# Four more FFN units by half-size products, token sums beside the first half, and low weight parts by adding transfers

## The chip, the cores and the metric

One core of one Trainium2 chip runs the whole model in one launch. The metric is the device time of that launch in microseconds (us). The kernel before takes 1629.13 us, the median of 3 runs (1628.31 to 1630.39). Every time in this document that is read from a profile comes from one profiled execution.

## The reference, cut to what matters

Two layers act on 256 latent tokens (LAT) and 256 context tokens (CTX) of width 1024. Layer 0 is a half FFN, an attention and a half FFN; layer 1 a half FFN, an mLSTM and a half FFN. Each part is followed by a layer norm, and each is modulated by vectors that come from products with `ada_w`.

```python
def half_ffn(h, shift, scale, gate, w_in, w_out, g, b):
    xm = modulate(h, shift, scale)
    a, u = jnp.split(xm @ w_in, 2, axis=-1)
    y = (jax.nn.silu(a) * u) @ w_out
    return post_norm(h, 0.5 * gate * y, g, b)
...
    for i in range(DEPTH):
        mod_lat = jnp.split((jax.nn.silu(c) @ ada_w[i] + ada_b[i])[:, None, :], N_MOD, axis=-1)
```

`w_in` is 1024 x 5632 and `w_out` 2816 x 1024, all float32. The output is the latent part of the last norm.

## The kernel before

The stages run one after the other: FFN 0, attention, FFN 1 (the second), FFN 2 (the third), mLSTM, last FFN. The change touches the second and the third, both `ffn` with `li` 1 and 2.

**Products.** A float32 product is made of three matmuls of a faster type: each operand is split into a high and a low part, and `mm3` (L241) issues high x high, high x low and low x high. `split` makes the parts of a tile: the high one by a cast on ScalarE (ACT, L225), the low one by a subtraction on VectorE (DVE, L230). `raw` (L210) loads a 512 KB chunk of weights by SP's queue into one of 3 slots, `pair` takes one of 7 tiles for both parts, and `chunk` does all three.

**An FFN.** The 2816 hidden columns are 22 units of 128, in two halves of 11; a unit has a silu side and a plain side, two chunks of `w_in`. Units 0 to 3 (the lead) run first for LAT and then for CTX, beside the end of the norm before. Units 4 to 10 are plain: 48 matmuls of 512 columns each. Then the out half 0 adds the eleven units' share to all 8 output blocks d (`unit_out`, 33 matmuls each). The second half, units 11 to 21, is fast: `fast_in` computes each unit by seven half-size products in place of eight (12 matmuls of 256 columns each, 84 in all), with `a11`, `a12`, `a21`, `a22` the quarters of the unit's weights. It needs four sums of quarters (`s1`, `s2`, `s4`, `s3`, L641, in one tile `sums`) and their splits, and three sums of halves of the tokens, which `fast_sums` (L611 to L623) makes for all fast units at once, beside d = 4 and 5 of the out half 0 (`SUMSAT`). One of these sums overwrites the CTX part of the lower half of `xh` and `xl`, which no plain unit reads any more by then. The out half 1 follows, its last four blocks (the tail) first for LAT and then for CTX, so that the next norm can begin.

**Dots.** The modulation vectors are dots on VectorE (`ada_dot`, L350): a 512 KB piece of `ada_w`, in one of 4 buffers, against two vectors (layer 1's last pieces against one). `DOTS` says how many pieces are loaded after each unit and each block; the dots of the pieces loaded at one such place are issued at the next (`flush`). `residual` (L563, L564) rescales the stream's blocks, two per unit.

**Order.** The Tile scheduler fixes one order for each engine and places the waits. An engine takes its instructions strictly in that order. So what stands ahead of an instruction on its own engine delays it even where the two have nothing to do with each other.

Of the kernel before, what the change touches and what calls it, by code (L numbers as in the profile page):

```python
# [18 lines left out]
P = 128  # L19
# [42 lines left out]
S1B = 5  # L62
# [26 lines left out]
SUMSAT = 4  # L89
# [53 lines left out]
class Stream:  # L143


    def __init__(self, b, chunks, sh=0):
        self.b, self.chunks, self.kept = b, chunks, (None, None)
        self.sh = sh if callable(sh) else lambda c: sh

    def __call__(self, i, w=P):  # L150
        c, o = divmod(i * P, 1024)
        if self.kept[0] != c:
            self.kept = (c, self.b.chunk(self.chunks[c], self.sh(c)))
        h, l = self.kept[1]
        return h[:, o : o + w], l[:, o : o + w]


class Keep(Stream):


    def __init__(self, b, chunks, sh=0, seen=None):
        super().__init__(b, chunks, sh)
        self.all = dict([seen.kept]) if seen else {}

    def __call__(self, i, w=P):
        c, o = divmod(i * P, 1024)
        if c not in self.all:
            self.all[c] = self.b.chunk(self.chunks[c], self.sh(c))
# [4 lines left out]
class Body:  # L173
    def __init__(self, ctx, tc, a, out):
# [8 lines left out]
        self.nraw, self.spare = 0, None  # L183

# [33 lines left out]
    def chunk(self, src, sh=0):  # L218
        r = self.raw(src)
        h, l = self.pair(sh=sh)  # L220
        self.split(r, h, l)
        return h, l

# [65 lines left out]
    def silu_c(self):  # L289

        pool = ExitStack()
        self.n += 1
        p = pool.enter_context(self.tc.tile_pool(name=f"cp{self.n}", bufs=1, side="right"))
        self.cp = p
        self.cb = self.t([P, 2, D], pool=p)
        return pool
# [5 lines left out]
    def silu_all(self):  # L302
        pool = self.silu_c()
        self.silu_load()
        self.silu()
        return pool
# [33 lines left out]
    def ada_load(self, layer, dt):  # L340
        if (layer, dt // ND) not in self.mod:
            self.mod[layer, dt // ND] = self.t([P, 2, ND])
        r = self.t([P, 1024], tag="ada", bufs=PIECES, pool=self.cp)
# [248 lines left out]
    def fast_operands(self, st):  # L592

        n = ND // 2 * TL
        x = self.t([P, 6 * n], F32R, pool=st)
        self.t([P, FLIP], pool=st)
        self.made = [[x[:, (2 * i + p) * n : (2 * i + p + 1) * n].rearrange("p (k f) -> p k f", f=TL) for p in range(2)] for i in range(3)]

    def fast_sums(self, i):
# [5 lines left out]
        def at(ks, g):  # L605
            return self.xh[:, ks, g[0] : g[1]], self.xl[:, ks, g[0] : g[1]]

        def whole(ks, g):
            o = self.tmp().rearrange("p (k f) -> p k f", k=2)
            h, l = at(ks, g)  # L610
            V.tensor_tensor(out=o, in0=h.bitcast(F32), in1=l.bitcast(F32), op=ALU.add)  # L611
# [3 lines left out]
        V.tensor_tensor(out=a, in0=a, in1=b, op=ALU.subtract)  # L615
        self.split(a, *at(lo, CTX))
# [3 lines left out]
        V.scalar_tensor_tensor(a, a, -1.0, c, ALU.mult, ALU.subtract)  # L620
        self.split(a, *made(0))
        d = whole(up, LAT)
        V.scalar_tensor_tensor(d, a, -1.0, d, ALU.mult, ALU.subtract)  # L623
        self.split(d, *made(2))

    def fast_in(self, j, w_in, st):
# [14 lines left out]
        add = lambda o, x, y: V.tensor_tensor(out=o, in0=x, in1=y, op=ALU.add)  # L641
# [7 lines left out]
        self.split(sums[:, : 2 * half], *ws[2])  # L649
        self.split(sums[:, 2 * half :], *ws[3])  # L650
# [33 lines left out]
    def ffn(self, layer, s, gate, groups, side, start=None, cpool=None):  # L684
# [4 lines left out]
        with self.tc.tile_pool(name=f"ffn{li}", bufs=1) as gp:  # L689
# [33 lines left out]
            stream = lambda j: Stream(self, [w_in[2 * j + i] for i in range(2)])  # L723
            for hf in range(2):
                js = list(range(hf * NFH, (hf + 1) * NFH))[0 if hf else done :]
                if hf == 0 and not start:
                    first = js[:LEAD]
                    ws = {j: Keep(self, [w_in[2 * j + i] for i in range(2)], SH) for j in first}
# [1040 lines left out]
```

## Time and profile before

| | |
|---|---|
| median of 3 runs | 1629.13 us (1628.31 to 1630.39) |
| span of the profiled execution | 1625.5 us |
| time around that span, against the median | 3.6 us |
| TensorE (PE) busy | 1606.9 us, 99% |
| VectorE (DVE) busy | 1355.7 us, 83% |
| ScalarE (ACT) busy | 749.2 us, 46% |
| GpSimd (POOL) busy | 63.0 us, 4% |
| moved by DMA | 251.56 MB |

The span runs from the first to the last recorded instruction. In a row of a timeline stand the start, the duration, the engine, the line of the program, the operation, output and inputs with their sizes, how many such instructions follow each other, and in brackets the idle time before and what ended it. A duration on VectorE or ScalarE overlaps the next instruction a little: the distance between two starts is what an instruction costs.

### The profile page before, as it was taken

What the parts mean: (1) busy time and instruction counts of PE and PEld (TensorE: products, weight loads), DVE (VectorE), ACT (ScalarE), POOL (GpSimd) and SP (SyncE); (2) the same over time, 40 slices, a digit from 0 to 9 for tenths busy, and PEclk for the clock granted to TensorE, in tenths of its full rate; (3) what the DMA queues carried; (4) which work ended last, traced back from release to release, by engine and by line L of the source; (5) the groups of instructions that cost most, each with busy time, mean ns of one, the idle gap of its engine ahead of it and who ended that gap; (6) DMA issues with size and microseconds to landing.
All of it is one profiled execution on the core that took longest, in us unless ns stands there. A gap on an engine that the chain in (4) does not pass through costs nothing. (4 is left out here: it accounts for less than half of the span.)

```text
span 1625.5 us, 26587 instructions
## 1 busy us (share of the span) xinstructions
PE 1606.9 (99%) x10304; PEld 1451.7 (89%) x10304; DVE 1355.7 (83%) x2699; ACT 749.2 (46%) x1272; POOL 63.0 (4%) x77
## 2 busy tenths in 40 slices
PE   9999999999999999999999999999999999999998
PEld 7888888889988998889998998889999989999987
DVE  7899977649889879899986879699966968897687
ACT  6522132314676443316652444336652657566542
POOL 0000000001011100000000100000001000030000
PEclk9999999999999999999999999999999999999999
DMA  9687766422202447633445258713363343437552
GB/s 358 221 252 237 235 205 187 137 66 85 66 1 80 151 134 221 219 117 105 129 146 180 79 165 289 253 58 118 104 225 100 98 130 87 142 110 253 181 176 91
DMA packets 72222, 251.56 MB, mean 155 GB/s; under 512 B 7960, under 2 KB 10776, under 8 KB 72096
## 3 DMA queue, kind: packets, MB, share of 16 engines
q1 hardware_dynamic: 71520, 249.09, 47.7%
q8 instruction: 80, 1.31, 0.3%
q10 hardware_dynamic: 576, 0.79, 0.1%
q14 instruction: 46, 0.38, 0.1%
HBM read 248.79 MB, written 1.05 MB: 154 GB/s over the span
## 5 line engine op out<-in xcount | busy, mean ns | idle before, releaser
L241 PE MATMUL t<-t,t 128*128 128x256 f32 (+2 forms) x8412 | 1317.0, 318 | 6.4 <-ACT t L225 3.3
L241 PEld LDWEIGHTS t<-t,t 128*128 128x128 f32 x8412 | 1185.7, 188 | 125.4 <-ACT t L225 4.7
L225 ACT CAST t<-t 128x1024 fp32r<-128x1024 f32 (+3 forms) x521 | 428.5, 844 | 485.8 <-PE t L241 214.5
L230 DVE TENSOR_TENSOR t<-t,t 128x256 fp32r<-128x256 f32 (+2 forms) x740 | 513.8, 729 | 111.9 <-ACT t L225 107.7
L350 DVE SCALAR_TENSOR_TENSOR t<-t,t 128x1024 bf16<-128x1024 f32 x224 | 260.7, 1220 | 0.0
L588 ACT ACTIVATE t<-t 128x512 f32<-128x512 f32 (+1 forms) x71 | 34.5, 490 | 103.5 <-PE t L241 102.4
L941 PE MATMUL t<-t,t 128*128 128x256 f32 (+1 forms) x256 | 79.3, 310 | 0.0
L718 DVE SCALAR_TENSOR_TENSOR t<-t,t,t 128x256 f32<-128x256 f32 x96 | 42.7, 478 | 43.9 <-PE t L241 43.7
L943 PE MATMUL t<-t,t 128*128 128x256 f32 (+1 forms) x256 | 78.4, 306 | 0.0
L942 PE MATMUL t<-t,t 128*128 128x256 f32 (+1 forms) x256 | 78.4, 306 | 0.0
L589 DVE TENSOR_TENSOR t<-t,t 128x512 f32<-128x512 f32 (+1 forms) x71 | 39.0, 553 | 40.6 <-PE t L241 28.1
L484 POOL TENSOR_TENSOR t<-t,t 128x256 f32<-128x256 f32 x30 | 23.4, 781 | 1104.9 <-ACT t L474 1103.5
L869 PE MATMUL t<-t,t 128*128 128x512 f32 (+1 forms) x300 | 60.5, 364 | 0.0
L869 PEld LDWEIGHTS t<-t,t 128*128 128x128 f32 x300 | 51.5, 189 | 8.9
L474 ACT ACTIVATE t<-t 128x256 f32<-128x256 f32 x72 | 26.1, 412 | 65.5 <-DVE t L467 65.5
L1456 PE MATMUL t<-t,t 128*128 128x512 f32 (+2 forms) x276 | 55.6, 356 | 0.0
L1456 PEld LDWEIGHTS t<-t,t 128*128 128x128 f32 (+1 forms) x276 | 44.9, 183 | 10.9 <-issue 0.9
L942 PEld LDWEIGHTS t<-t,t 128*128 128x128 f32 x256 | 48.1, 188 | 3.0 <-DVE t L230 0.5
L941 PEld LDWEIGHTS t<-t,t 128*128 128x128 f32 x256 | 48.3, 189 | 2.7
L943 PEld LDWEIGHTS t<-t,t 128*128 128x128 f32 x256 | 48.1, 188 | 2.5
L541 ACT ACTIVATE t<-t,t 128x256 fp32r<-128x256 f32 x72 | 32.8, 503 | 30.1 <-DVE t L540 30.1
L641 DVE TENSOR_TENSOR t<-t,t 128x512 f32<-128x512 f32 x66 | 45.2, 685 | 0.4
(206 smaller groups left out, 1078.6 us busy)
## 6 DMA issues: line engine op xcount, KB each, us to landing
t<-in_ffn_in SPq DMA_DIRECT2D x168, 512.0 KB, 4.1
t<-in_ada_w SPq DMA_DIRECT2D x138, 512.0 KB, 4.4
t<-in_ffn_out SPq DMA_DIRECT2D x66, 512.0 KB, 4.5
t<-in_ffn_last SPq DMA_DIRECT2D x22, 512.0 KB, 3.5
t<-in_att_in SPq DMA_DIRECT2D x12, 512.0 KB, 3.5
t<-in_att_out SPq DMA_DIRECT2D x8, 512.0 KB, 3.6
t<-in_ml_qk SPq DMA_DIRECT2D x8, 512.0 KB, 3.6
t<-in_ml_v SPq DMA_DIRECT2D x8, 512.0 KB, 3.5
```

What stands on the lines that cost most here:

```text
L225: self.behind(self.nc.scalar.copy(h, x))
L230: self.behind(self.nc.vector.tensor_tensor(out=ls, in0=xs, in1=hs.bitcast(F32), op=ALU.subtract))
L241: mm = lambda *k, **kw: self.nc.tensor.matmul(*k, skip_group_check=not group, **kw)
L350: ins = nc.vector.scalar_tensor_tensor(self.tmp().bitcast(BF16), r, 1.0, self.cb[:, v, :], ALU.mult, ALU.mult, accum_out=to)
L589: V.tensor_tensor(out=sl, in0=sl, in1=pu[:, :n], op=ALU.mult)
L641: add = lambda o, x, y: V.tensor_tensor(out=o, in0=x, in1=y, op=ALU.add)
L718: V.scalar_tensor_tensor(z, y[:, gg[0] - t0 : gg[1] - t0], gate()[:, v, d : d + 1], z, ALU.mult, ALU.add)
L869: pin(nc.tensor.matmul(o, gs[g], ws[k][w][:, i : i + n], start=k == k0 and g == w == 0, stop=k == k1 - 1 and g == 1,))
L941: mm(o, self.xh[:, k, c], wh, start=k == 0, stop=False)
L942: mm(o, self.xh[:, k, c], wl, start=False, stop=False)
L943: mm(o, self.xl[:, k, c], wh, start=False, stop=k == ND - 1)
L1456: mm = lambda *k, **kw: pin(nc.tensor.matmul(*k, **kw))
```

## The change

- `FASTAT` = 7: units 7 to 10 of the second and third FFN are fast too, so 15 units in place of 11.
- `fast_sums` runs beside units 4 and 5. Since units 5 and 6 still read the CTX half of `xh` and `xl`, the first token sum is kept in four tiles (`first`, tag s1) and split into place by `fast_first` after unit 6. Tag s1 has 4 buffers in place of 5.
- `added` makes the low part of a tile without VectorE: ScalarE casts to the high part (L233), ScalarE writes its negative (L234), and GpSimd issues a transfer (L235) that reads the weights from memory once more and adds them. It serves lead units 1 to 3, plain units 4 to 6 and the fast units but 11 and 12 (`PLAIN`): 38 tiles in an FFN, 25 of them full and 13 half chunks.
- The four weight sums are four `tmp` tiles, split in halves; the `sums` tile is gone.
- The `ada_w` buffers are given back after unit 4, where the waiting dots are flushed; in the out half 0 the pieces use the halves of one weight tile. `DOTS` has 2 pieces after units 0 to 2 and none later in the first half. In the second FFN 2 after d = 0 to 6 and 3 after each block of the out half 1; in the third 2 or 3 after d = 0 to 6 and 4 after each block of the out half 1.
- The scratch for GpSimd's transfers is 1024 in place of 512.

```diff
-S1B = 5
+S1B = 4
...
-SUMSAT = 4
+FASTAT = 7
+PLAIN = (NFH, NFH + 1)
...
-    1: {**{("in", j): 2 for j in range(11)}, **{("out", 0, d): 2 if d < 2 else 1 for d in range(4)}, **{("out", 1, d): 1 for d in range(4)}},
-    2: {**{("in", j): 2 for j in range(4)}, **{("in", j): 3 if j < 9 else 2 for j in range(4, 11)}, **{("out", 0, d): 2 if d < 3 else 0 for d in range(4)},
-        **{("out", 1, d): 2 if d < 3 else 1 for d in range(4)}},
+    1: {**{("in", j): 2 for j in range(3)}, **{("out", 0, d): 2 for d in range(7)}, **{("out", 1, d): 3 for d in range(4)}},
+    2: {**{("in", j): 2 for j in range(3)}, **{("out", 0, d): 2 for d in range(3)}, **{("out", 0, d): 3 for d in range(3, 7)},
+        **{("out", 1, d): 4 for d in range(4)}},
...
+    def added(self, x, h, l, src):
+
+        S = self.nc.scalar
+        S.copy(h, x)
+        S.activation(l, h.bitcast(F32), AF.Copy, scale=-1.0)
+        self.nc.gpsimd.dma_start(l, src.bitcast(F32R), accum_op=ALU.add)
...
         a, b = whole(lo, LAT), whole(lo, CTX)
-        V.tensor_tensor(out=a, in0=a, in1=b, op=ALU.subtract)
-        self.split(a, *at(lo, CTX))
+        for k in range(2):
+            o = self.first[2 * i + k] = self.t([P, TL], tag="s1", bufs=S1B)
+            V.tensor_tensor(out=o, in0=a[:, k, :], in1=b[:, k, :], op=ALU.subtract)
         c = whole(up, CTX)
         V.tensor_tensor(out=b, in0=c, in1=b, op=ALU.subtract)
         self.split(b, *made(1))
...
-    def fast_in(self, j, w_in, st):
+    def fast_first(self):
+        for k in range(ND // 2):
+            self.split(self.first[k], *self.x(k, CTX))
+
+    def fast_in(self, j, w_in):
...
-        sums = self.t([P, 4 * half], tag="sums", bufs=1, pool=st)
...
-        s1, s2, s4, s3 = (part(sums, i) for i in range(4))
+        s1, s2, s4, s3 = (self.tmp() for _ in range(4))
...
-        self.split(a11, *ws[0])
-        self.split(r1, *ws[1])
+        if j in PLAIN:
+            self.split(a11, *ws[0])
+            self.split(r1, *ws[1])
+        else:
+            self.added(a11, *ws[0], w_in[2 * j, :, :half])
+            self.added(r1, *ws[1], w_in[2 * j + 1])
...
-        self.split(sums[:, : 2 * half], *ws[2])
-        self.split(sums[:, 2 * half :], *ws[3])
+        for i, x in enumerate((s1, s2, s4, s3)):
+            self.split(x, *(part(y, i % 2) for y in ws[2 + i // 2]))
...
+                    if fast and j >= FASTAT:
+                        self.fast_in(j, w_in)
+                    else:
+                        unit_in(j, stream(j), allg)
+                        if j >= LEAD + FAFTER:
+                            self.fine = False
+                        call("in", j)
                     assert not self.running
...
                     self.residual(2, self.pin)
+                    if fast and j == LEAD:
+                        self.flush()
+                        self.shut()
+                        self.cp = None
+                        self.fast_operands()
+                    if fast and LEAD <= j < LEAD + 2:
+                        self.fast_sums(j - LEAD)
+                    if fast and j == FASTAT - 1:
+                        self.fast_first()
```

What this does to the order shows at three places. The first is VectorE in the third FFN, where the lead ends. Before, 14 dots (L350, t_9761 to t_9800) end with the row that stands first here; then come unit 4's product with its silu (L589), a chunk's split and the product's split.

```order
L350 SCALAR_TENSOR_TENSOR t_9800,t_9765<-t_9792,t_8495 128x1024
L589 TENSOR_TENSOR t_9874<-t_9874,t_9807 128x512
L230 TENSOR_TENSOR t_10110<-t_10108,t_10110 128x1024
L230 TENSOR_TENSOR t_9873<-t_9874,t_9872 128x512
L350 SCALAR_TENSOR_TENSOR t_9879,t_9765<-t_9802,t_8495 128x1024
```

Changed, 18 dots (L371) end with the first row here; behind them are unit 4's product (L610) and the token sums of `fast_sums` (L631, L637) beside its split (L243).

```order
L371 SCALAR_TENSOR_TENSOR t_10122,t_10087<-t_10114,t_5457 128x1024
L610 TENSOR_TENSOR t_10188<-t_10188,t_10125 128x512
L631 TENSOR_TENSOR t_10203<-t_67,t_68 128x512
L631 TENSOR_TENSOR t_10205<-t_67,t_68 128x512
L243 TENSOR_TENSOR t_10187<-t_10188,t_10186 128x512
L584 SCALAR_TENSOR_TENSOR t_66<-t_66,t_9349,t_9347 128x256 x2
L637 TENSOR_TENSOR t_10207<-t_10203,t_10205 128x256
```

The run of dots is four longer, and what follows it now includes all of `fast_sums`. Further down in the changed order the parts of the first token sum are written (t_68 is `xl`), and then the first two weight sums of unit 7 (L666) and the low part of the first (t_10411) are made.

```order
L243 TENSOR_TENSOR t_68<-t_10207,t_67 128x256
L243 TENSOR_TENSOR t_68<-t_10209,t_67 128x256
L243 TENSOR_TENSOR t_68<-t_10302,t_67 128x256
L243 TENSOR_TENSOR t_68<-t_10304,t_67 128x256
L666 TENSOR_TENSOR t_10405<-t_10401,t_10403 128x512
L666 TENSOR_TENSOR t_10406<-t_10405,t_10401 128x512
L243 TENSOR_TENSOR t_10411<-t_10405,t_10411 128x512
```

So unit 7's first weight sum stands 59 rows behind the first dot; before, unit 7 had no such sum.

The second place is VectorE in the second FFN, where out half 0 goes over to unit 11. Before, the first weight sums of unit 11 (L641, output t_7153) stand between the steps of `fast_sums` and ahead of the update by the last block (L718).

```order
L641 TENSOR_TENSOR t_7153<-t_7149,t_7151 128x512
L230 TENSOR_TENSOR t_6935<-t_7046,t_6935 128x512
L230 TENSOR_TENSOR t_6935<-t_7044,t_6935 128x512
L623 SCALAR_TENSOR_TENSOR t_7059<-t_7044,t_7059 128x512
L641 TENSOR_TENSOR t_7153<-t_7153,t_7149 128x512
L641 TENSOR_TENSOR t_7153<-t_7149 128x512
L230 TENSOR_TENSOR t_6935<-t_7059,t_6935 128x512
L718 SCALAR_TENSOR_TENSOR t_66<-t_7064,t_6753,t_66 128x256 x2
```

Changed, they (L666, outputs t_7348 and t_7349) stand behind that update (L747) and four dots.

```order
L747 SCALAR_TENSOR_TENSOR t_66<-t_7292,t_6960,t_66 128x256 x2
L371 SCALAR_TENSOR_TENSOR t_7333,t_7236<-t_7289,t_5457 128x1024
L371 SCALAR_TENSOR_TENSOR t_7335,t_7236<-t_7289,t_5457 128x1024
L371 SCALAR_TENSOR_TENSOR t_7337,t_7236<-t_7289,t_5457 128x1024
L371 SCALAR_TENSOR_TENSOR t_7339,t_7236<-t_7289,t_5457 128x1024
L666 TENSOR_TENSOR t_7348<-t_7344,t_7346 128x512
L666 TENSOR_TENSOR t_7349<-t_7348,t_7344 128x512
L243 TENSOR_TENSOR t_7354<-t_7348,t_7354 128x512
```

The update by the last block and the four dots are now ahead of unit 11's sums.

The third place is ScalarE in the second FFN between unit 7 and unit 8. Before, between the silu of unit 7 and that of unit 8 (L588), stand the cast of unit 7's result, two casts of chunks and the residual.

```order
L588 ACTIVATE t_6434<-t_6372 128x512
L225 CAST t_6432<-t_6434 128x512
L225 CAST t_6712<-t_6710 128x1024
L225 CAST t_6741<-t_6739 128x1024
L564 ACTIVATE t_66<-t_66,t_5379 128x256 x2
L588 ACTIVATE t_6517<-t_6455 128x512
```

Changed, unit 7's copies and silu (L700, L705) stand between cast (L233) and negation (L234) of unit 8's two tiles: t_6515 is a11's, t_6516 the second chunk's, and t_6517 a sum's.

```order
L233 CAST t_6515<-t_6507 128x512
L234 ACTIVATE t_6515<-t_6515 128x512
L700 COPY t_6405<-t_6402 128x256
L233 CAST t_6516<-t_6509 128x1024
L238 CAST t_6517<-t_6511 128x512
L705 ACTIVATE t_6405<-t_6405 128x512
L234 ACTIVATE t_6516<-t_6516 128x1024
L238 CAST t_6517<-t_6512 128x512
```

The negation of t_6516, after which its transfer can be issued, is behind the cast of a sum and the silu of unit 7.

More of the change, by code (lines that the diff above doesn't have):

```diff
@@ L722, in ffn @@
             w_in, w_out = self.a["ffn_in"][li], self.a["ffn_out"][li]
-            stream = lambda j: Stream(self, [w_in[2 * j + i] for i in range(2)])
+            stream = lambda j: Stream(self, [w_in[2 * j + i] for i in range(2)], add=range(2) if fast else ())
             for hf in range(2):
@@ L727, in ffn @@
                     first = js[:LEAD]
[L728 removed]
+                    ws = {j: Keep(self, [w_in[2 * j + i] for i in range(2)], SH, add=range(2) if j else ()) for j in first}
                     assert len(self.running) == 1
```

100 lines of the change are left out of this document (48 added, 52 removed).

## The prediction

> **What bounds the kernel now.** The profile's page comes first: its span, and its busy times by engine.
>
> ```profile
> span 1625.5 us, 26587 instructions
> PE 1606.9 (99%) x10304; PEld 1451.7 (89%) x10304; DVE 1355.7 (83%) x2699; ACT 749.2 (46%) x1272; POOL 63.0 (4%) x77
> ```
>
> TensorE is busy 99% of the span, so time can fall where matmuls go, and it rises by whatever makes TensorE wait. The median, 1629.13 us, is 3.6 us above this span; I carry that 3.6 along. Next, busy time by stretches of the second FFN, with columns for each engine: plain units 7 to 10, the out half 0 beside which the token sums run, and eight fast units of the second half.
>
> ```profile
> core 0: us, PE busy (x) PEld busy (x) DVE busy (x) ACT busy (x) POOL busy (x), PEclk, DMA share, GB/s
> 640.00:682.00 42.00, 42.00 (x187) 34.80 (x186) 38.05 (x62) 16.22 (x24) 0.00 (x0) 1.00 0.72 228
> 690.00:747.00 57.00, 57.00 (x273) 48.04 (x272) 55.98 (x99) 17.74 (x24) 0.00 (x0) 1.00 0.35 107
> 765.00:841.00 76.00, 76.00 (x673) 76.00 (x672) 71.85 (x95) 49.82 (x83) 0.00 (x0) 1.00 0.40 124
> ```
>
> TensorE has no gap in any of the three, at a granted clock of 1.00: there is no wait to win back here. VectorE stands at 91%, 98% and 95%: the second engine in line, with almost no room. What a unit costs TensorE is the distance between two silus, which each unit has once. From ScalarE's timeline, plain units of the first half (L588) and fast ones (L676):
>
> ```profile
> 649.18 0.60 ACT L588 ACTIVATE t<-t 128x512 f32<-128x512 f32 x1 [1.45 <-PE t L241]
> 660.07 0.60 ACT L588 ACTIVATE t<-t 128x512 f32<-128x512 f32 x1 [1.66 <-PE t L241]
> 791.18 0.62 ACT L676 ACTIVATE t<-t 128x512 f32<-128x512 f32 x1
> 800.70 0.63 ACT L676 ACTIVATE t<-t 128x512 f32<-128x512 f32 x1
> ```
>
> A plain unit takes 10.89 us and a fast one 9.52.
>
> **Part 1: fewer matmuls.** Four units in each of two FFNs become fast: 8 x (10.89 - 9.52) = 10.9 us less, all on TensorE, the engine that is busy throughout. That is the whole possible gain.
>
> **Part 2: token sums and dots ahead of unit 7.** Unit 7 now needs the token sums and its own weight sums. All of it is VectorE work, in a fixed order, behind a run of dots (the L350 rows below; L371 in the changed kernel). VectorE's timeline in the third FFN, where the lead ends:
>
> ```profile
> 954.90 0.75 DVE L230 TENSOR_TENSOR t<-t,t 128x256 fp32r<-128x256 f32 x2
> ...
> 959.43 1.56 DVE L230 TENSOR_TENSOR t<-t,t 128x1024 fp32r<-128x1024 f32 x2 [0.64 <-ACT t L225]
> 960.91 1.22 DVE L350 SCALAR_TENSOR_TENSOR t<-t,t 128x1024 bf16<-128x1024 f32 x1
> ...
> 976.95 0.08 DVE L350 DVE_READ_ACCUMULATOR t<-t,t 128x1 f32 x1
> 976.95 0.68 DVE L589 TENSOR_TENSOR t<-t,t 128x512 f32<-128x512 f32 x1
> 977.55 1.81 DVE L230 TENSOR_TENSOR t<-t,t 128x1024 fp32r<-128x1024 f32 x2
> 979.29 1.21 DVE L350 SCALAR_TENSOR_TENSOR t<-t,t 128x1024 bf16<-128x1024 f32 x1
> ...
> 983.88 0.86 DVE L563 SCALAR_TENSOR_TENSOR t<-t,t,t 128x256 f32<-128x256 f32 x2
> ```
>
> And ScalarE's first silu after the lead, with what it waited for; and the loads of the dots' pieces, from the page's table of transfers (KB, and median us to landing last):
>
> ```profile
> 957.95 0.39 ACT L588 ACTIVATE t<-t 128x256 f32<-128x256 f32 x1 [1.39 <-PE t L241]
> t<-in_ada_w SPq DMA_DIRECT2D x138, 512.0 KB, 4.4
> ```
>
> Fourteen dots fill 960.91 to 976.95: 1.147 us each. A 512-wide operation takes 0.60 (976.95 to 977.55), a 1024-wide subtraction 1.14 (977.55 to 979.29, less 0.60), a 256-wide one 0.36 (0.75 for a pair with its tail), an update of the residual 0.44; the 256-wide scalar-tensor ones I take at 0.40. ScalarE's row says when TensorE ended the lead: about 957.9.
>
> Now 18 dots stand there. The lead's last split needs no 1024-wide subtraction any more, so they start about 959.8 and end 18 x 1.147 later, at 980.4. Up to the low part of unit 7's first weight sum the order puts 27 operations of 0.60, 6 of 0.44, 4 of 0.40 and 8 of 0.36: 16.2 + 2.6 + 1.6 + 2.9 = 23.3 us, so it is ready at 1003.8. TensorE wants it after units 4 to 6 (3 x 10.88) and three half-size products (9.52 / 7 = 1.36 each, twelve matmuls of 0.113; 4.1), plus two matmuls: at 994.9. It waits 8.9 us. The nine pieces behind the dots come through SP's queue as before: one is read in 2.3 us and loaded in 4.4 with four in flight, so none is late. In between nothing can step ahead, since the order is fixed; unit 4's product waits behind the dots too, as it does today, without harm. The second FFN has 12 dots at this place, 6 x 1.147 = 6.9 us less: a wait of 2.0. Together 10.9, which eats part 1 alone.
>
> **Part 3: dots in the out halves.** Unit 11 follows d = 7 of out half 0. ScalarE's first copy of unit 11, then VectorE's updates by the out products (L718), in the second FFN:
>
> ```profile
> 743.76 0.38 ACT L666 COPY t<-t 128x256 f32<-128x256 f32 x1 [0.36 <-PE t L241]
> 742.71 0.87 DVE L718 SCALAR_TENSOR_TENSOR t<-t,t,t 128x256 f32<-128x256 f32 x2
> ...
> 862.33 0.88 DVE L718 SCALAR_TENSOR_TENSOR t<-t,t,t 128x256 f32<-128x256 f32 x2 [1.57 <-PE t L241]
> 863.13 0.75 DVE L424 TENSOR_TENSOR t<-t 128x256 f32<-128x256 f32 x2
> 885.08 0.48 DVE L718 SCALAR_TENSOR_TENSOR t<-t,t,t 128x256 f32<-128x256 f32 x1 [2.94 <-PE t L241]
> ...
> 888.97 0.48 DVE L718 SCALAR_TENSOR_TENSOR t<-t,t,t 128x256 f32<-128x256 f32 x1 [2.94 <-PE t L241]
> ```
>
> The first two rows put unit 11's start at about 742.4 (one product of 1.36 us ends just before the copy, d = 7 just before the update); its first weight sum and its low part stand ahead of that now. Changed, they come behind the update (0.2 + 0.8 us), four dots of d = 6 (4.6) and three operations of 0.60: 7.4 us after the start, where 4.3 is wanted: 3.1 us lost, in the third FFN with three dots 1.9. In the second FFN's out half 1, 18 dots (before 6) stand between 862.33 and the split of the chunk that d = 6 of the tail reads: 18 x 1.147 + 2 pairs of sums at 0.7 and 2 further steps come to 26.5 us, so 888.8 against 887.3 wanted (885.0, when d = 5 ended, plus 20 matmuls of 0.113): 1.6 us. The third FFN has 12 there and room. At its end 4 dots are flushed where 1 was, ahead of the next norm: 0 to 3.4 us; I take 0, since a tail piece of TensorE (3.9 us, 885.08 to 888.97) covers three dots, and keep 3.4 for the range. Parts 2 and 3: 10.9 + 5.0 + 1.6 = 17.5 us.
>
> **Part 4: low parts by an adding transfer.** For 38 tiles in each FFN, VectorE's subtraction (1.14 us) goes. Instead ScalarE negates and GpSimd issues a transfer that adds the weights from memory. No row shows such a transfer; its time from negated tile to landed sum, L, decides. The nearest rows are plain loads (median us to landing last):
>
> ```profile
> t<-in_ffn_in SPq DMA_DIRECT2D x168, 512.0 KB, 4.1
> t<-in_att_in SPq DMA_DIRECT2D x12, 512.0 KB, 3.5
> t<-in_start_in SPq DMA_DIRECT2D x8, 448.0 KB, 6.3
> t<-in_start_in SPq DMA_DIRECT2D x1, 512.0 KB, 9.1
> t<-in_const SPq DMA_DIRECT2D x2, 256.0 KB, 2.7
> L225 ACT CAST t<-t 128x1024 fp32r<-128x1024 f32 x27 | 28.4, 1053 | 12.4 <-PE t L241 11.2 <-DVE t L641 1.1 <-DMA t<-in_ffn_out 0.2
> 600.62 0.39 ACT L588 ACTIVATE t<-t 128x256 f32<-128x256 f32 x1 [1.41 <-PE t L241]
> 606.04 0.39 ACT L588 ACTIVATE t<-t 128x256 f32<-128x256 f32 x1 [1.39 <-PE t L241]
> ```
>
> I take L = 4.1, the same tensor at the same size, with ends 2.7 and 9.1. The Trainium skill, in "DMA: Bandwidth & Descriptors", section "Anatomy of one DMA — SWDGE (gpsimd) path", fits a GpSimd-issued transfer as 2.0 us plus bytes over 436 GB/s; an estimate from it is 3.2 us for 512 KB, and the sum below would be 1645 by it. No run here shows it for an adding one.
>
> Three places have less cover than the chain needs. A 1.05 us cast and a negation like it stand ahead of L everywhere.
> - Lead unit 3's second chunk gets its tile one pass of a 256-wide unit before use (5.4 us between the last two rows, 5.2 left with the overlap): 5.2 - 2.1 = 3.1 for L, so L - 3.1 is lost, in both FFNs: 2.0.
> - Unit 8's second chunk loads into the slot that unit 7's last sum frees, about 6.7 us after unit 7 starts; landing takes 4.1, cast, unit 7's silu and negation 2.7, and then L, while unit 8 wants the low part some 12.5 after unit 7's start. ScalarE's casts of unit 8's sums stand behind. About L is lost, at least 3 (the cast alone is late): 8.2 for two.
> - Unit 13, the first with the transfer after two without: ScalarE's chain leaves 1.9 for L; 4.4 for two.
>
> Between fast units the chain has some 7.5 us for L (9.52 less cast and negation, about one unit ahead), so the rest is hidden. The bytes fit: 0.75 MB more in 9.52 us are 79 GB/s on top of the 124 of the fast units' window, less than the 228 of the plain one. Part 4: 14.6 us. With L at 2.7: 0 + 6.0 + 1.6 = 7.6; at 6.3: 6.4 + 12.6 + 8.8 = 27.8.
>
> **The sum.** 1625.5 - 10.9 + 17.5 + 14.6 = 1646.7 us, plus 3.6: 1650 us. With L from 2.7 to 6.3, 1643 to 1664.
>
> **The rivals.**
> 1. VectorE gets ahead, and the gain stays. Each FFN loses 25 subtractions of 1.14 and 13 of 0.60, some 36 us of VectorE. For: TensorE's 99%, and VectorE's 91 to 98% that would fall. Against: the relief comes in units 8 to 10 and 13 to 21, not in the 37 us between the lead and unit 7's first sum. It decides if that sum is ready within 37 us, that is if the dots are taken beside it, and L is below 3: 1629.1 - 10.9 = 1618, up to 1624 with small waits. Chance 0.13.
> 2. Waits and gain cancel: L is covered everywhere and only part 2 is lost, 10.9 against 10.9: 1629, within 0.2% (3.3 us, about what a measurement of this kernel can tell). Against: unit 8's chain above is late for any L. Chance 0.08.
> 3. The adding transfers are slow because GpSimd and VectorE get in each other's way. Two timelines, VectorE and GpSimd, in a norm of before:
>
> ```profile
> 557.04 1.84 DVE L542 SCALAR_TENSOR_TENSOR t<-t,t,t 128x256 fp32r<-128x256 f32 x2
> 560.65 1.26 DVE L542 SCALAR_TENSOR_TENSOR t<-t,t,t 128x256 fp32r<-128x256 f32 x3
> 554.60 4.00 POOL L521 TENSOR_TENSOR t<-t,t 128x256 f32<-128x256 f32 x4 [7.97 <-PE t L241]
> ```
>
> Beside GpSimd's four adds VectorE's step takes 0.92 us, alone 0.42. If issuing suffers likewise, L goes to 6.3 (1664); at 9.1 the three places cost 12.0 + 18.2 + 14.4, and each of some 20 fast units 1.6 more: 1625.5 - 10.9 + 17.5 + 76.6 + 3.6 = 1712. Chance 0.17, with the lower end likelier. The Trainium skill, "SBUF — State Buffer", says that a transfer issued by GpSimd waits for its descriptors while VectorE holds the shared port, about 3.1 us in place of 0.62 in its example; the rows above agree that the two engines share something, but no row shows it for descriptors.
>
> **How the numbers follow.** The forecast (gain, VectorE's waits and L near 4) has 0.62, and gives 1650. The range takes in L from 2.7 to 6.3, half of the VectorE waits being wrong by a few us (down to 1630), half of rival 1 and of rival 3: 1622 to 1676. Faster 0.14 (rival 1 and a little), same 0.08, slower 0.78.
>
> **What would show it.** TensorE's busy time down by about 11 us while its span share falls to 97% or less; in unit 7 of the third FFN a TensorE gap near 9 us released by VectorE's sums, near 2 in the second; gaps of 2 to 3 us at unit 11; gaps released by GpSimd's transfers in units 8 and 13 of both. The adding transfers' median to landing should be near 4 us. The prediction is wrong if unit 7 of the third FFN starts without a gap, or if L is over 7.5 and every fast unit waits.

## The result, and the profile after

The changed kernel takes 1712.5 us (1709.4 to 1717.7, 4 runs) against 1628.9: a ratio of 1.052, 95% interval 1.050 to 1.054. It is slower, as forecast, but by 84 us where 21 were forecast, and outside the range. First the page's span, busy times, the queue that only GpSimd's adding transfers use, and the groups and transfers that are new.

```profile
span 1707.8 us, 27521 instructions
PE 1634.2 (96%) x10592; PEld 1484.3 (87%) x10592; DVE 1333.0 (78%) x2687; ACT 837.9 (49%) x1456; POOL 128.3 (8%) x153
...
q0 software_dynamic: 10944, 33.04, 11.1%
...
L235 POOL DMA_DIRECT2D t<-in_ffn_in x76 | 66.5, 875 | 560.1 <-ACT t L702 186.4
...
t<-in_ffn_in SPq DMA_DIRECT2D x168, 512.0 KB, 4.5
t<-in_ffn_in POOLq DMA_DIRECT2D x50, 512.0 KB, 6.9
t<-in_ffn_in POOLq DMA_DIRECT2D x26, 256.0 KB, 4.9
```

TensorE's idle time rose from 18.6 to 73.6 us, and its busy time by 27 us. That second number is the odd one: by count its work fell by 10.9 us (more but narrower matmuls), so some 38 us are matmuls that ran slowly. By the starts of the matmuls some 22 of them lie in stretches at a granted clock of 0.50; the others come at 1.00. VectorE is less busy than before. An adding transfer of 512 KB lands 6.9 us after its issue, where 4.1 was taken. What TensorE waited for between the second FFN's lead and the third FFN's end (sum, times, longest) was:

```profile
PE t L254 <- DMA t<-in_ffn_in: 23.3, 8, 5.0
PE t L254 <- ACT t L238: 15.2, 5, 6.5
PE t L254 <- ACT t L695: 6.7, 12, 1.1
```

The first row is the adding transfers. The second is a cast that stands behind VectorE's late sums, the third a copy held up on ScalarE. The places follow from the starts of the matmuls, 84 to a fast unit. Each cell is the time beyond a full-pace unit (9.52 us) or beyond the kernel before, in the second and the third FFN:

| place | forecast | measured |
|---|---|---|
| gain of matmuls, both | -10.9 | -10.9 |
| lead (the third FFN's with the tail before it) | 1.0, 1.0 | 3.9, 4.4 |
| unit 7 | 2.0, 8.9 | 5.8, 13.0 |
| unit 8 | 4.1, 4.1 | 8.6, 8.9 |
| units 9 and 10 | 0, 0 | 0.9, 0.5 |
| unit 11 (9.80 before) | 3.1, 1.9 | 4.9, 2.7 |
| unit 12 | 0, 0 | 0.6, 0.7 |
| unit 13 | 2.2, 2.2 | 8.8, 8.5 |
| units 14 to 21 | 0, 0 | 6.5, 6.2 |
| out half 1 of the second FFN | 1.6 | 1.0 |
| end of the third FFN, norm, mLSTM's start | 0 | 5.5 |
| sum | 21 | 81 |

Nearly every place was named. All but one of the named places (the out half 1) cost more than their price, and two that were priced at nothing cost 12.7 and 5.5 us.

What stretched each long wait shows in the windows around the gap of the second FFN's unit 13: the gap, the matmuls after it, and those behind these.

```profile
core 0: us, PE busy (x) PEld busy (x) DVE busy (x) ACT busy (x) POOL busy (x), PEclk, DMA share, GB/s
783.60:788.80 5.20, 0.35 (x3) 0.15 (x2) 2.90 (x5) 2.92 (x4) 1.76 (x2) 0.92 1.03 219
788.80:793.50 4.70, 4.70 (x22) 4.70 (x23) 0.00 (x0) 0.00 (x0) 0.00 (x0) 0.50 0.69 115
793.50:799.00 5.50, 5.50 (x45) 5.50 (x45) 3.80 (x7) 3.98 (x9) 0.00 (x0) 0.88 0.30 100
```

After five idle microseconds the granted clock is 0.50 in a window of 4.7 us: 22 matmuls where 41 fit, and a few more slow ones behind it, so the gap of 5.1 us costs some 7.5. The Trainium skill, "TensorE: Matmul & The Clock Gate", section "Part 1: The HAM clock gate", states that TensorE falls to half its clock after an idle window of about 3.4 us and needs about as long of work to come back. This trace agrees on the half clock, but not on the length of the idle time, and there the measurement decides: in the second and third FFN and the norm behind them gaps of 2.5 us and more, some of them shorter than 3.4, are followed by 16 to 27 slow matmuls in nine of ten cases (once, after 2.95 us, by none), and gaps of 1.0 to 1.6 by none of their own. In other versions gaps of 1.4 to 2.0 us are followed by them too (e7, and e1 beside e10). The kernel before has no gap above 2.0 us outside its start, and no such stretch in the two FFNs.

### The profile page after: what moved, and what is told of

Same layout as the page of the kernel before. It is cut to its first block, busy times and chain, and to the rows that moved or that the text cites. A ratio compares the mean times of both kernels' runs of the same rounds, so it can differ in the third digit from the quotient of the medians.

```text
span 1707.8 us, 27521 instructions
## 1 busy us (share of the span) xinstructions
PE 1634.2 (96%) x10592; PEld 1484.3 (87%) x10592; DVE 1333.0 (78%) x2687; ACT 837.9 (49%) x1456; POOL 128.3 (8%) x153
## 3 DMA queue, kind: packets, MB, share of 16 engines
q0 software_dynamic: 10944, 33.04, 11.1%
## 4 chain that ended last, share of the span: by engine, by line
PE 69%; DVE 10%; issue 9%; DMA 8%; ACT 4%; DVEq 0%; POOLq 0%; SPq 0%; POOL 0%; ACTq 0%
PE t L254 53%; DMA t<-in_ffn_in 6%; PE t L1483 4%; PE t L896 4%; DVE t L243 3%; PE t L969 2%; PE t L968 2%; PE t L970 2%; ACT t L238 2%; DMA t<-in_ffn_out 2%; DVE t L666 1%; PE t L468 1%; DVE t L371 1%; ACT t L233 1%; DVE t L561 1%
## 5 line engine op out<-in xcount | busy, mean ns | idle before, releaser
L254 PE MATMUL t<-t,t 128*128 128x256 f32 (+2 forms) x8700 | 1343.6, 316 | 59.3 <-DMA t<-in_ffn_in 26.4
L254 PEld LDWEIGHTS t<-t,t 128*128 128x128 f32 x8700 | 1217.9, 192 | 172.5 <-DMA t<-in_ffn_in 29.5
L238 ACT CAST t<-t 128x512 fp32r<-128x512 f32 (+2 forms) x525 | 385.4, 755 | 439.0 <-PE t L254 163.6
L243 DVE TENSOR_TENSOR t<-t,t 128x512 fp32r<-128x512 f32 (+3 forms) x672 | 453.4, 704 | 183.0 <-ACT t L238 181.7
L371 DVE SCALAR_TENSOR_TENSOR t<-t,t 128x1024 bf16<-128x1024 f32 x224 | 260.4, 1220 | 2.3 <-DMA t<-in_ada_w 2.3
L235 POOL DMA_DIRECT2D t<-in_ffn_in x76 | 66.5, 875 | 560.1 <-ACT t L702 186.4
L233 ACT CAST t<-t 128x512 fp32r<-128x512 f32 (+1 forms) x76 | 68.6, 902 | 38.5 <-DMA t<-in_ffn_in 23.6
L610 DVE TENSOR_TENSOR t<-t,t 128x256 f32<-128x256 f32 (+1 forms) x63 | 33.6, 536 | 67.6 <-ACT t L609 34.7
L609 ACT ACTIVATE t<-t 128x256 f32<-128x256 f32 (+1 forms) x63 | 29.8, 477 | 106.9 <-PE t L254 91.1
L234 ACT ACTIVATE t<-t 128x512 fp32r<-128x512 f32 (+1 forms) x76 | 69.4, 913 | 1.2
L747 DVE SCALAR_TENSOR_TENSOR t<-t,t,t 128x256 f32<-128x256 f32 x96 | 42.6, 478 | 32.4 <-PE t L254 32.2
L666 DVE TENSOR_TENSOR t<-t,t 128x512 f32<-128x512 f32 x90 | 61.9, 687 | 4.5 <-DMA t<-in_ffn_in 3.4
L896 PEld LDWEIGHTS t<-t,t 128*128 128x128 f32 x300 | 51.5, 189 | 8.9
L1483 PEld LDWEIGHTS t<-t,t 128*128 128x128 f32 (+1 forms) x276 | 44.9, 183 | 11.1 <-issue 1.2
L495 ACT ACTIVATE t<-t 128x256 f32<-128x256 f32 x72 | 25.8, 410 | 55.7 <-DVE t L488 55.7
L969 PEld LDWEIGHTS t<-t,t 128*128 128x128 f32 x256 | 48.1, 188 | 4.4 <-DVE t L243 1.9
```

The source lines that it names most:

```text
L233: S.copy(h, x)
L234: S.activation(l, h.bitcast(F32), AF.Copy, scale=-1.0)
L238: self.behind(self.nc.scalar.copy(h, x))
L243: self.behind(self.nc.vector.tensor_tensor(out=ls, in0=xs, in1=hs.bitcast(F32), op=ALU.subtract))
L254: mm = lambda *k, **kw: self.nc.tensor.matmul(*k, skip_group_check=not group, **kw)
L371: ins = nc.vector.scalar_tensor_tensor(self.tmp().bitcast(BF16), r, 1.0, self.cb[:, v, :], ALU.mult, ALU.mult, accum_out=to)
```

## The experiments

**Theory A**: the adding transfers' chain and VectorE's late work make TensorE wait at the places named, and each long wait is followed by a stretch at half clock. The rivals are named with each run. Edits are against the changed kernel unless another is named. e1 to e10 ran once each and e11 to e14 twice, while four runs of the changed kernel lie 8 us apart: so differences of a few us between two times say little, and the readings go by places in the profiles.

**e1, no adding transfers.**

```diff
     def added(self, x, h, l, src):
-        S.copy(h, x)
-        S.activation(l, h.bitcast(F32), AF.Copy, scale=-1.0)
-        self.nc.gpsimd.dma_start(l, src.bitcast(F32R), accum_op=ALU.add)
+        self.split(x, h, l)
```

> The changed kernel with every low part made by the cast and VectorE's subtraction again, no adding transfer; the rest as changed. Theory A (the adding transfers' chain, cast, negation, 6.9 us to landing, makes TensorE wait in lead unit 3, units 8 and 13 and from unit 16 on, and each long wait is followed by some 4 us at half clock): those losses go, 4 + 5 in the leads, 17.5 in units 8, 17.3 in units 13, about 13 in the later fast units, together some 55 us; VectorE gets back 36 us of work in each FFN, which makes unit 7 a few us later. 1660 to 1675, units 8 and 13 at 9.5 to 10. Rival B (VectorE is the bound, the transfers only stand where it would be late anyway): units 8 and 13 stay at 18 us or the loss moves to the units beside them, 1700 or more.

1657.1 us. Unit 13 is 9.52 in both FFNs and units 14 to 21 too but for one in each, of 9.9 and 10.0; unit 8 is 11.1 and 9.5; unit 7 is still 12.8 and 21.9 (15.4 and 22.6 changed). So 55 of the 84 us are the adding transfers, although VectorE is busy 72 us longer without them. B falls. What e1 still waits for:

```profile
PE t L252 <- DVE t L241: 13.3, 7, 9.9
PE t L252 <- ACT t L236: 6.0, 3, 2.6
```

One wait of 9.9 us behind VectorE's subtractions is unit 7 of the third FFN.

**e2, short dots.**

```diff
-            self.tmp().bitcast(BF16), r, 1.0, self.cb[:, v, :], ALU.mult, ALU.mult, accum_out=to
+            self.tmp().bitcast(BF16)[:, :64], r[:, :64], 1.0, self.cb[:, v, :64], ALU.mult, ALU.mult, accum_out=to
```

> The changed kernel with each dot over the first 64 of 1024 columns (15/16 of every dot is left out; all loads, places and order rules stay). Theory A says that the dots only matter ahead of unit 7, of unit 11 and of the mLSTM's norm: unit 7 falls to 10 us or less in both FFNs (15.4 and 22.6 now), unit 11 to about 10 (14.7 and 12.5), the stretch behind the third FFN's tail by 4; units 8 and 13 keep their 18 us. About 1712 - 6 - 13 - 5 - 2.5 - 4 = 1682. Rival B (VectorE's total is the bound): units 8, 13 and the later fast units fall too, 1650 or less. Rival C (the token sums are late even without the dots): unit 7 of the third FFN stays above 15.

1687.1 us. Unit 11 is 10.1 and 10.2, and the stretch behind the third FFN's out half 1 is 65.2 us (69.8 changed, 65.6 before): the dots cost there what they were said to. VectorE is busy 216 us less, and units 8 and 13 still take 17 us, so B falls. But unit 7 only falls to 13.8 and 19.2, which is C's sign. VectorE's rows in the third FFN's lead say why, with the idle time ahead of a dot in brackets:

```profile
1001.41 0.23 DVE L371 SCALAR_TENSOR_TENSOR t<-t,t 128x64 bf16<-128x64 f32 x1 [8.78 <-DMA t<-in_ada_w]
...
1004.62 0.23 DVE L371 SCALAR_TENSOR_TENSOR t<-t,t 128x64 bf16<-128x64 f32 x1 [2.83 <-DMA t<-in_ada_w]
```

With only four buffers, pieces five to nine arrive when SP's queue gets to them, whatever a dot costs. So this run doesn't settle C, nor what the run of dots costs there; e13 does.

**e3 and e4, what the transfer moves.** e3 adds 16 columns alone, e4 copies in place of adding.

```diff
-        self.nc.gpsimd.dma_start(l, src.bitcast(F32R), accum_op=ALU.add)
+        self.nc.gpsimd.dma_start(l[:, :16], src[:, :16].bitcast(F32R), accum_op=ALU.add)    # e3
+        self.nc.gpsimd.dma_start(l, src.bitcast(F32R))                                     # e4
```

> The changed kernel with each adding transfer over the first 16 columns alone (the rest of the low part is left as the negated high part, so the bytes are left out and the chain of cast, negation, issue and landing stays). Theory A: landing falls from 6.9 us to 2.5 or so, so units 8 and 13 lose some 4.4 us less each and their half-clock stretch partly (18 to 12 us), the leads about 2 each, and the later units some 1 us each as loads land sooner: 1712 - 4 x 6 - 4 - 10 = about 1675. Rival D (bytes do not matter, only the chain through ScalarE's and GpSimd's queues does): units 8 and 13 stay near 18, no more than 5 us in all.

> The changed kernel with the same transfers from GpSimd, same tiles and bytes, but copying in place of adding (the low part is then the weight itself). The order of every engine is the same. Theory A: landing time comes from the issue, the bytes and the other loads in flight, not from the addition: 512 KB still land in 6 to 7 us and the time is within 5 us of the changed kernel. Rival E (the addition makes the transfer slow: it must read the tile and write it back): landing falls to about 4.5 us and the time by 15 to 30 us.

1662.6 and 1675.9 us. The transfers of e3, and then of e4:

```profile
t<-in_ffn_in POOLq DMA_DIRECT2D x76, 8.0 KB, 2.3
```

```profile
q0 software_dynamic: 10944, 33.04, 6.5%
...
t<-in_ffn_in POOLq DMA_DIRECT2D x50, 512.0 KB, 4.5
t<-in_ffn_in POOLq DMA_DIRECT2D x26, 256.0 KB, 3.3
```

Copying lands like a plain load (4.4 in that run), so GpSimd's issue is not slow: the addition makes it 6.9. That is rival E, and worth 37 us here; my own expectation for e4 failed. The first of these rows says the same: the packets of the same 33.04 MB take 6.5% of the 16 engines' span where the adding ones took 11.1%. With hardly any bytes (e3), units 14 to 21 are 9.52 throughout, units 8 and 13 still 12 to 14: the chain's fixed part. With all bytes but copied (e4), units 14 to 21 are 9.52 too, but for four of 9.9 to 10.2. D falls; e3's time is 12 us below theory A's. The Trainium skill, "DMA: Bandwidth & Descriptors", section "Anatomy of one DMA — SWDGE (gpsimd) path", gives 2.0 us plus bytes over 436 GB/s, by estimate 3.2 us for 512 KB. Beside the other loads the copy took 4.5 and the adding one 6.9, so the measurement decides.

**e5 and e6, a fourth slot for loads, and its control.**

```diff
-RAW = 3
+RAW = 4                                      # e5; e6 keeps 3
...
-        x = self.t([P, 6 * n], F32R, pool=st)
+        x = self.t([P, 4 * n], F32R, pool=st)
-        self.made = [[x[:, (2 * i + p) * n : (2 * i + p + 1) * n].rearrange("p (k f) -> p k f", f=TL) for p in range(2)] for i in range(3)]
+        self.made = [[x[:, (2 * i + p) * n : (2 * i + p + 1) * n].rearrange("p (k f) -> p k f", f=TL) for p in range(2)] for i in (0, 0, 1)]
```

> The changed kernel with four slots for loaded weights in place of three; to make room two of the three token sums share one tile (so the output is not the reference's; the work is the same). Theory F (units 16 to 21 run at 10.2 to 11.2 us because the second chunk's load waits for the slot that the last sum of the unit before frees, lands 5 to 6 us later beside an adding transfer, and ScalarE stands still behind its cast): units 16 to 21 fall to 9.52, unit 8 and unit 13 lose 3 to 4 us, about 1712 - 12 - 12 = 1688. Rival G (DMA bandwidth or the adding transfers' landing sets their pace): the later units stay above 10, within 5 us of the control e6.

> The control for e5: three slots as in the changed kernel, and the two token sums share one tile as in e5. All theories: within 4 us of the changed kernel, 1708 to 1716, with the same unit times.

1690.6 and 1705.5 us; the control is a little below its 1708 to 1716. In the changed kernel units 17 to 21 of the second FFN take 10.2 to 11.2 us. ScalarE's rows in unit 19:

```profile
850.36 0.63 ACT L705 ACTIVATE t<-t 128x512 f32<-128x512 f32 x1 [0.41 <-DVE t L704]
853.37 1.05 ACT L233 CAST t<-t 128x1024 fp32r<-128x1024 f32 x1 [2.38 <-DMA t<-in_ffn_in]
854.32 0.37 ACT L695 COPY t<-t 128x256 f32<-128x256 f32 x1
```

The cast waits 2.38 us for its load, and the copy for which TensorE waits stands behind it. With four slots (e5) every unit from 14 on is 9.52 in both FFNs, though a 512 KB adding transfer takes 7.5 us to land there. So their pace was set by the loads' slots (theory F), and G falls. Units 8 and 13 hardly answer: against e6, unit 8 of the third FFN falls by 1.2 us and unit 13 of the second by 2.0, and the other two rise by 1.0 and 0.3, so that part of theory F's expectation failed.

**e7, work in the gap.**

```diff
+        if j in (FASTAT + 1, NFH + 2):
+            e = self.ps()[:, :TL]
+            for k in range(32):
+                self.pin(self.nc.tensor.matmul(e, w["a11"][0][:, :P], self.x(0, LAT)[0], start=k == 0, stop=k == 31, skip_group_check=True))
         product(y, "a12", of(ND // 2, LAT), True, True)
```

> The changed kernel with 32 more matmuls of 256 columns (3.6 us, nobody reads their sums) in units 8 and 13 of both FFNs, just ahead of the first matmul that waits for an adding transfer. Theory H (after a gap of over some 2.5 us TensorE runs about 20 to 27 matmuls at half its pace, which costs 2 to 2.6 us a time): the gap of 4.4 to 5.3 us falls under 2, no half-pace stretch follows, units 8 and 13 go from 18.2 to about 16, the time falls by some 8 us though work is added: 1704. Rival I (the slow stretch has another cause, such as the arrival of the weights): the slow stretch stays, the time is the same or some us longer.

1704.5 us. In unit 13 it does what H says: 15.7 and 15.4 us where 18.4 and 18.0 were, with 32 matmuls more. The windows of unit 13 in the second FFN (columns as above), the added matmuls, the rest of the gap, and what follows:

```profile
782.20:786.00 3.80, 3.80 (x36) 3.80 (x35) 3.77 (x7) 3.77 (x6) 0.89 (x1) 1.00 1.04 268
786.00:788.10 2.10, 0.35 (x4) 0.15 (x2) 0.22 (x1) 0.02 (x1) 0.87 (x1) 1.00 1.05 198
788.10:792.80 4.70, 4.70 (x41) 4.70 (x42) 1.03 (x2) 1.73 (x4) 0.00 (x0) 1.00 0.74 123
```

The last row holds 41 matmuls at a clock of 1.00, where the same 4.7 us held 22 at 0.50. In unit 8 it failed (18.6 and 20.6 us): a gap of 2.0 us still lies ahead of the added matmuls in the second FFN and one of 4.5 behind them in the third, and slow matmuls follow both. The time is the 1704 that H named, but by luck: the four units together lose only 2.8 us.

**e8, e12, e13, fewer dots in the third FFN's lead.** On e1:

```diff
-    2: {**{("in", j): 2 for j in range(3)}, **{("out", 0, d): 2 for d in range(3)}, **{("out", 0, d): 3 for d in range(3, 7)},
+    2: {**{("out", 0, d): 2 for d in range(3)}, **{("out", 0, d): 3 for d in range(3, 7)},
...
-    later = [(1, p, both2) for p in range(40)] + [(1, p, (0,)) for p in range(40, 72)]
+    later = [(1, p, both2) for p in range(40)] + [(1, p, (0,)) for p in range(40, 66)]
+    b.mod[1, 8] = b.t([P, 2, ND])            # e13: after the third FFN
+    nc.vector.memset(b.mod[1, 8], 0.0)
```

> e1 (no adding transfers) with no pieces of ada_w loaded after the lead of the third FFN, so 6 dots stand ahead of unit 4's work and the token sums in place of 18. The last 6 of 72 pieces are left out (one gate of the last FFN is then zero, so the output is not the reference's). Theory A: the third FFN's unit 7 was late by the run of 18 dots; 12 of 1.147 us less make its sums 13.8 us earlier, so unit 7 falls from 21.9 to about 10, unit 8 may take a few us of it: 1657 - 11 = 1646. Rival C (token sums and the splits of units 4 to 7 fill VectorE anyhow): unit 7 stays above 15.

> e8 once more, since all of its run, stages that no edit touches too, was 2.5 to 6% longer than the others. Theory A as for e8: unit 7 of the third FFN about 9.7 to 10, 1646. Rival C: unit 7 above 15.

> e8's edit (no ada_w pieces after the lead of the third FFN, 6 dots there in place of 18, the last 6 pieces left out, so the output is not the reference's) with the tile for the missing gate made after the third FFN in place of at the start, so that no other tile's place in SBUF moves before that. Theory J (the early tile of 64 bytes per partition moved all tiles behind it, and matmuls read and write at other offsets more slowly): a fast unit is 9.52 again, unit 7 of the third FFN 9.5 to 10, about 1646. Rival K (fewer dots there slow the matmuls in some other way): 9.97 stays, 1677.

1678.4, 1677.2 and 1655.7 us. Unit 7 of the third FFN is 10.3, 10.3 and 10.1 us in place of 21.9 in all three: the twelve dots (and their loads) were its wait. C falls. But e8 and e12 are slower than e1 as a whole. A fast unit takes 9.97 to 10.08 us in them, and matmuls are slower from the first FFN on. e13, with the missing gate's tile made late, has units of 9.52 and of 9.89; those at 9.89 (some 6 us) and the two out halves 0, each 1.7 us longer than in e1, are most of why it is not at 1646.

**e14, the early tile alone,** on e1:

```diff
+    nc.vector.memset(b.t([P, 2, ND]), 0.0)
```

> e1 with one more tile of 64 bytes per partition made at the start and set to zero once, which nobody reads; the rest and the order are those of e1 (1657). Theory J: every fast unit takes 9.97 in place of 9.52 and 512-wide matmuls 0.233 in place of 0.227, 1657 + 3 to 4% of 1100 us = about 1690. Rival K: 1657, 9.52.

1682.8 us, 26 more than e1, for a tile that nobody reads. The 512-wide matmuls of the first FFN, in a window of 80 us, in e1 and then in e14 (busy, mean ns):

```profile
L252 PE MATMUL t<-t,t 128*128 128x512 f32 x341 | 77.5, 389 | 0.0
L1481 PE MATMUL t<-t,t 128*128 128x512 f32 x14 | 3.3, 389 | 0.0
```

```profile
L252 PE MATMUL t<-t,t 128*128 128x512 f32 x329 | 76.9, 395 | 0.0
L1481 PE MATMUL t<-t,t 128*128 128x512 f32 x16 | 3.9, 396 | 0.0
```

The two lines together are 355 matmuls in e1 and 345 in e14, at a granted clock of 1.00 in both. K falls: where tiles lie in SBUF changes the matmuls' pace. It does not change it everywhere: the out halves 0 take what they take in e1.

**e9, adding transfers in the kernel before:** `added` for lead units 1 to 3, units 4 to 6 and fast units 13 to 21.

> The kernel before, with one part of the change alone: low parts by adding transfers in lead units 1 to 3, units 4 to 6 and fast units 13 to 21 of the second and third FFN (60 tiles); fast units, sums and dots stay as before. Theory A (an adding transfer of 512 KB lands in about 7 us, late wherever its chain starts anew, and lets later fast units run behind their loads): leads 4 to 5 us longer, unit 13 about 8.7 longer in both, units 16 to 21 about 1 us longer each: 1629 + 9 + 17 + 13 = 1668. Rival B (VectorE, relieved of 36 us in each FFN, gives time back, and the transfers were only late beside the other edits): 1640 or less.

1689.3 us, 61 more than before and 21 more than expected: B falls. But the waits are not where theory A put them: unit 13 takes 9.5 and 10.0 us, unit 14 17.9 and 12.5, later units up to 14.0, and the two leads, with the norms ahead of them, 8.2 and 16.8 us more than before. And e9 is not the change's transfers alone. It kept the scratch of 512 that the kernel before has for GpSimd's transfers, where the change has 1024. In e9 no transfer is issued before the one ahead of it has landed (54 of 59 within 0.4 us of that); in the changed kernel 48 of 75 are. The scratch is the likely reason, though no run varied it alone. So e9 shows that adding transfers cost a lot here too, but not that the change's own would cost 61 us without the other edits; e1 is the run for that. In the lead of the third FFN the late issue shows. TensorE, ScalarE's last negation, and GpSimd:

```profile
956.81 1.44 PE L458 MATMUL t<-t,t 128*128 128x1 f32 x6 [7.92 <-POOL t L495]
```

```profile
940.73 1.06 ACT L232 ACTIVATE t<-t 128x1024 fp32r<-128x1024 f32 x1
```

```profile
947.90 0.89 POOL L233 DMA_DIRECT2D t<-in_ffn_in  x1 [6.22 <-PE t L252]
953.53 0.87 POOL L233 DMA_DIRECT2D t<-in_ffn_in  x1 [4.73 <-issue]
954.09 2.67 POOL L495 TENSOR_TENSOR t<-t,t 128x256 f32<-128x256 f32 x3
```

The norm's adds (L495) stand on GpSimd behind a transfer (L233). Its negation had ended by 941.8, but it is issued only at 953.53 ("issue": the profile shows nothing that it waited for), 0.3 us after the one of 947.90 has landed, and TensorE waits 7.9 us for the adds.

**e10, without both,** on e1: `FASTAT = 11`, so units 7 to 10 are plain.

> The changed kernel without adding transfers and with units 7 to 10 plain again: what is left is the moved dots, the token sums beside units 4 and 5 and the split of the sums in halves. Theory A: no wait in units 7 to 10 (43.5 us for the four), and what the moved dots cost stays: unit 11 some 4 to 5 us late in both FFNs, the second FFN's end and the next lead 3.6, the third FFN's end and the norm 6: 1629 + 9 + 4 + 6 = 1648. Rival C (the early sums with their dots cost by themselves, by VectorE's load): units 4 to 10 take longer than before, 1655 or more.

1653.2 us. The second FFN's units 4 to 10 take what they took before. In unit 7 of the third, which is plain here, TensorE waits 4.1 us for a chunk's subtraction behind the 18 dots and the token sums (6.0 us with the slow stretch):

```profile
1011.93 2.56 PE L252 MATMUL t<-t,t 128*128 128x512 f32 x7 [4.12 <-DVE t L241]
```

So A missed that one, and C holds for this place. Unit 11 (4.9 and 2.5), the tail with the next lead (2.1) and the third FFN's end (6.0) cost as named; six units of the second FFN at 9.89 to 9.93 make most of the rest.

e1 and e10 also show that the length of a wait alone doesn't settle what follows it. In both, unit 11 of the third FFN waits 1.42 us at the same matmul. The 3.4 us that begin 1.6 us behind it, in e1 and then in e10 (columns as above):

```profile
1119.70:1123.10 3.40, 3.40 (x18) 3.40 (x17) 2.95 (x6) 2.08 (x5) 0.00 (x0) 0.50 0.75 261
```

```profile
1117.20:1120.60 3.40, 3.27 (x28) 3.07 (x28) 2.94 (x6) 2.59 (x7) 0.00 (x0) 1.00 0.73 255
```

18 matmuls at half clock in e1, 28 at the full one in e10; the unit takes 13.5 and 12.3 us.

**e11, one more plain unit,** on e1: `FASTAT = 8`.

> e1 (no adding transfers) with unit 7 plain too, so that units 8 to 10 are the new fast ones. Theory A (unit 7's inputs are a fixed chain of VectorE work behind the lead): 10.9 us more for that chain against 1.4 of gain given up and one more pair of splits on VectorE in each FFN; units 7 to 10 fall from 43.1 to about 41 in the second FFN and from 51.8 to about 44 in the third: 1657 - 10 = 1647. Rival B (VectorE's total is the bound): the wait moves to units 8 to 10 whole, 1655 or more.

1652.5 us (ratio 1.015 to before, 1.011 to 1.019). Units 7 to 10 fall from 43.1 to 41.0 and from 51.8 to 47.6. The first is as A says, the second half of it: the wait of e10's place is there again, 4.3 us.

## Why the prediction was wrong

- **Direction and places: right.** TensorE had no wait to lose, so the gain was bounded by 10.9 us, and it came: units 9, 14 and 15 of the second FFN run at 9.52. Waits at unit 7, 8, 11 and 13 and in the leads ate it.
- **Part 4's L was mis-sized.** "I take L = 4.1, the same tensor at the same size": that row is a plain load. e4 has 4.5 for a copy by the same queue; the addition makes it 6.9 (and 8.5 us from issue to landing at unit 13 of the second FFN, by its chain of waits, beside other transfers). The range's upper end took in 6.3. The 37 us between e4 and the changed kernel hang on it. But put into the prediction's own sum, 6.9 makes Part 4 31.4 and the whole 1667, still inside the range; the next two steps make most of the rest of the miss. (The working for unit 8, 6.7 + 4.1 + 2.7 + L against 12.5, gives L + 1.0 and not L.)
- **A wait was priced by its length alone.** No step had the half clock behind it. Nine stretches at about 2 us make some 20 us; e7 shows the cause in unit 13. Unit 7 of the third FFN is this: its gaps are 8.4 us of idle time against 8.9 forecast, and the other 4.6 of its 13.0 are matmuls slower than the pace. The cast behind VectorE's sums ends the long ones:

```profile
1041.06 0.58 PE L254 MATMUL t<-t,t 128*128 128x256 f32 x1 [6.51 <-ACT t L238]
1042.01 1.43 PE L254 MATMUL t<-t,t 128*128 128x256 f32 x5 [0.37 <-DVE t L243]
1045.00 9.02 PE L254 MATMUL t<-t,t 128*128 128x256 f32 x52 [1.56 <-ACT t L238]
```

- **"Between fast units the chain has some 7.5 us for L, so the rest is hidden" failed,** not on L, but on the loads. The sum that frees a slot, the load into it, the cast and the next sum form a loop of their own; beside the adding transfers a load takes long enough to make it up to 11 us. e5 opens it with a fourth slot. e3 shows that without the bytes three are enough, and e4 that they are nearly so with the bytes copied.
- **Part 2 was right in kind.** e13 shows the twelve dots' wait gone. e2 adds what the working passed over: shorter dots gain only 3.4 us there, since the pieces behind the fourth come late as well.
- **Part 3**: unit 11 as named (e2). "At its end 4 dots are flushed where 1 was ... I take 0" failed. The chain of waits of the changed kernel has them ahead of the mLSTM's norm:

```profile
1341.81 4.58 DVE t L371 x8
1346.39 0.40 DVE t L1238
```

  That stretch takes 69.8 us where it took 65.6; the tail piece did not cover them, and TensorE's 2.5 us gap there was followed by a slow stretch of its own.
- **Rival 3** came close in size: its figure for L = 9.1, 1712, is the measured time. That is luck. Its L of 6.3 is nearest to 6.9, and its mechanism is not the one: e4's copies are issued by the same GpSimd beside the same VectorE and land in 4.5.

What is left open: why some 256-wide stretches run at 9.89 us a unit and not 9.52 (below), what decides whether a short wait is followed by half clock, and how much of e9's 61 us is its smaller scratch.

No version here beats the kernel before. There VectorE stands at 91 to 98% in these stretches; a fast unit costs it about 9.0 us (71.85 in eight) and a plain one without its dots about 5.4, and the one way tried to relieve it cost 55 us.

## What to carry to other kernels

Price a wait on a kernel bound by TensorE as its length plus the slow stretch behind it. Here waits of 2.5 us and more nearly always had one, and of those of 1.4 to 2.0 us some, so a short wait is not safe either. Don't price a transfer that computes by one that only moves. When one part of a change is tried alone, take along the settings it was given (e9's scratch). And where buffers are reused in a loop (slot freed, load, cast, sum), add the loop up on its own: hidden latency in one link shows in the pace as soon as the loop is longer than a unit.

## What the runs showed of the hardware

- Adding during a transfer costs time: 512 KB land in 6.9 us, copied by the same queue in 4.5; 256 KB in 4.9 against 3.3. In e9, where never two are in flight, 512 KB still take 6.6.
- Half clock after a gap: 22 matmuls in 4.7 us at a granted 0.50, and none of it in unit 13 when the gap was filled to under 2 us by useless matmuls (e7). Behind 1.97 us in e7's unit 8 and 1.42 us in e1 it came all the same; behind 1.42 us in e10 it didn't.
- 64 bytes more per partition in front of the other tiles make 512-wide matmuls 2.9% slower (0.233 us apart in place of 0.227, in a window of the first FFN; not in the out halves 0) and fast units 4.7% in the second FFN and 5.9% in the third (e14: 9.97 and 10.08 us), at an unchanged granted clock of 1.00.
- 256-wide matmuls have another pace, 9.89 us a unit in place of 9.52, with the tiles where they were. In e10 it sets in at unit 16 of the second FFN and lasts to the end of the half, at a granted clock of 1.00; in e1 units 17 to 21 are 9.52. The runs don't tell why.
